# A 512-column product for both parts of the tokens, and full tiles in the retention

## Chip, core and metric

The kernel runs on one core of one Trainium2 chip. The metric is device time in microseconds: the median of 3 runs was 1045.59 us (1044.72 to 1046.28).

## The reference

Two transformer-like blocks, one after the other, on 256 tokens of width 1024, all in float32. The first puts 16 learned tokens in front (272 tokens), normalises, projects with one wide matrix, and mixes two branches: a chunkwise retention with 8 heads (rotary q and k, a decay per head, a norm and a gate) and a gated linear recurrence behind a short convolution; both are projected, gated, added and projected again (`w_out`), with a residual. A gated feed-forward of width 2816 follows. The second block projects its normalised input for a gated linear attention (4 heads), a sparse attention that keeps the 64 best keys by an indexer's scores (8 heads), and an attention on 256 memory rows; three gates merge them, and a mixture of 16 experts (two chosen per token) ends the block.

In short, of each projection:

```
proj = u @ w_in                      # u: tokens x 1024, float32
s = einsum(q, k) * intra             # retention, per head and chunk
out = einsum(s, v) + cross           # cross: through the carried state
```

## The kernel before, in words

Tokens lie transposed: features in the 128 partitions (8 tiles of 128 for the width), tokens in the columns. Float32 accuracy is had from the fast float32r products by splitting every operand in a high and a low part: weights by `_emit` (a ScalarE copy to float32r at L268, a VectorE subtraction at L269), tokens by `split_act` (L299 and L300, with a scale L302 and L303). A projection is `ws` (L325): for each output tile of 128 features and each of its 8 input tiles k it issues three products into one PSUM tile of 128x512, of which 256 or 272 columns are used: weights high by tokens high (L342), weights high by tokens low (L343), weights low by tokens high (L344). Then it lets the running side jobs take a step (`self.step()`) and hands the PSUM tile to `evac`, which is the stage's own function and works on VectorE and ScalarE. `proj` (L356) calls `ws` for 256 output features, one "chunk" of weights, at a time. With `tail=n` the two output tiles of a chunk are first computed without the last n input tiles, and those are added at the end, so that the first products of a stage don't need the last tiles of the stage before.

Weights come by DMA from SP's queue as chunks of 1 MB, in two halves of 128x1024. `get` splits up to two chunks ahead (AHEAD = 2), and there are six buffers for high and six for low halves. PSUM has two pools of four tiles: `mm` for the projections and `sp` for all else. Small working tiles of at most 272 columns come from a pool of 12 buffers (`self.t`). The order of the instructions on each engine is set at build time by the framework's scheduler, from the program's order and costs and readiness that it reckons itself; where a side job is a generator, its parts are put into the program at `self.step()`, one part per output tile.

The stages in order, with the time in the profile at which they start: li (0), v, gb and the recurrence's gates (35), k and ga (99), q and g with the retention (148), lg (213), br_ret (237), br_lru (262), out1 (285), ffi (308), ffo (434), then in block 2 iq (496), sm, dq (514), dk and dv (548), gk and gq (558), gv (585), gg (607), gt0 with o_gla and gt1 with o_dsa (640), mk (745), mv (770), mq (792), gt2 (820), o_mem (856), out2 (879), and the experts (905 on).

In the retention each head has three score products: with the first chunk of 128 keys (L626), with the 16 leading tokens (L627, 16 output partitions), and with the second chunk (L628). Their results are scaled and masked to `sm`, `s1`, `s2` (L630 to L632). Later the head's output is summed from products with `sm` (L640, 16 rows), `s1` (L641) and `s2` (L643). These are plain float32 products; the profile shows two records for each.

`sp` and `mm` in a row's names are the two PSUM pools, `tmp` the small working tiles, `big` the large ones, `raw`, `hi` and `lo` the weights before and after the split.

Of the kernel before, what the change touches and what calls it, by code (L numbers as in the profile page):

```python
# [195 lines left out]


class _Build:
    def __init__(self, nc, tc, ctx, a):
# [21 lines left out]
    def bigt(self, dt=F32, shape=(P, KT, T1)):  # L221
        return self.big.tile(list(shape), dt, name=self.name("big"), tag="big")

    def t(self, n, dt=F32, tag=None):
# [99 lines left out]

    def ws(self, keys, x, evac, nk=(KT,), cols=slice(0, SEQ), ms=(P, P), bank=None, tail=0):  # L325


        nc = self.nc
        xh, xl = x
        chunks = [self.get(*k) for k in keys]  # L330
        tiles = [(c, kc) for c, n in enumerate(nk) for kc in range(n)]
        n, nt = cols.stop - cols.start, len(tiles)
        pss = [None] * len(ms)

        def products(j, ks):
            m, ps = ms[j], pss[j]
            for k in ks:
                c, kc = tiles[k]
                hi, lo = chunks[c][j]
                wh, wl = hi[:, kc * m:kc * m + m], lo[:, kc * m:kc * m + m]  # L340
                rh, rl = xh[:, k, cols], xl[:, k, cols]
                nc.tensor.matmul(ps[:m, :n], wh, rh, start=k == 0, stop=False)  # L342
                nc.tensor.matmul(ps[:m, :n], wh, rl, start=False, stop=False)  # L343
                last = nc.tensor.matmul(ps[:m, :n], wl, rh, start=False, stop=k == nt - 1)  # L344
            return last
        for j in range(len(ms)):
            if not tail or j == 0:
                for i in range(len(ms)) if tail else (j,):
                    pss[i] = (bank or self.mm)()
                    products(i, range(nt - tail))  # L350
            if tail:
                products(j, range(nt - tail, nt))
            self.step()
            evac(j, pss[j][:ms[j], :n])

    def proj(self, key, n, x, evac, cols=slice(0, SEQ), j0=0, bank=None, tail=0):  # L356

        for j in range(j0, j0 + n // 256):
            self.ws([(key, j)], x, lambda i, ps, j=j: evac(2 * j + i, ps), cols=cols, bank=bank,
                    tail=tail if j == j0 else 0)  # L360

# [70 lines left out]
    def block1(self):  # L432
# [11 lines left out]
        x = self.bigt()  # L444
        uh, ul = self.bigt(F32R), self.bigt(F32R)
        u = (uh, ul)
        self.prm = self.keep(NPRM)
# [117 lines left out]
        def turn_v(j, vf):  # L565
            pt = self.sp()
            for t in range(2):
                te.transpose(pt[:, t * P:t * P + P], vf[:, META + t * P:META + t * P + P], self.c("ident"))
            te.transpose(pt[:META, 2 * P:3 * P], vf[:, 0:META], self.c("ident"))
            act.copy(vt[:, :, j, :], pt[:, 0:2 * P].rearrange("p (t e) -> p t e", t=2))  # L570
            act.copy(vm[:META, j, :], pt[:META, 2 * P:3 * P])
        def ev_gate(dst):
# [7 lines left out]
        for j in range(4):  # L580
            if j:
                lru(j - 1)
            convolve(j)
            self.proj("v", 256, u, ev_v, cols=ALL, j0=j)
            self.proj("gb", 256, u, ev_gate(tb), cols=X, j0=j)

# [20 lines left out]
        for j in range(4):  # L607
            self.proj("k", 256, u, rot(k, ALL), cols=ALL, j0=j)
            self.proj("ga", 256, u, ev_gate(ta), cols=X, j0=j)
# [5 lines left out]
        yh, yl = self.bigt(F32R, (P, KT, SEQ)), self.bigt(F32R, (P, KT, SEQ))  # L615
        qd = self.c("qdec").rearrange("p (t h) -> p t h", t=2)
# [4 lines left out]
        def retention(h0):  # L621
            ss = self.s(4)
            parts = []
            for h in (h0, h0 + 1):
                pm, p1, p2 = self.sp(), self.sp(), self.sp()
                te.matmul(p1[:, :SEQ], k[:, h, META:META + P], q[:, h, :SEQ], start=True, stop=True)  # L626
                te.matmul(pm[:META, :SEQ], k[:, h, 0:META], q[:, h, :SEQ], start=True, stop=True)  # L627
                te.matmul(p2[:, :P], k[:, h, META + P:T1], q[:, h, P:SEQ], start=True, stop=True)  # L628
                sm, s1, s2 = self.t(SEQ), self.t(SEQ), self.t(P)
                act.mul(sm[:META, :], pm[:META, :SEQ], kd[:META, h:h + 1])  # L630
                v.scalar_tensor_tensor(s1, p1[:, :SEQ], kd[:, 8 + h:9 + h], self.c("tri1"), op0=ALU.mult, op1=ALU.mult)
                v.scalar_tensor_tensor(s2, p2[:, :P], kd[:, 16 + h:17 + h], self.c("tri"), op0=ALU.mult, op1=ALU.mult)  # L632
                parts.append((sm, s1, s2))
                yield
            po = self.sp()
            for h, (sm, s1, s2) in zip((h0, h0 + 1), parts):
                b = (h - h0) * 2 * P
                for t in range(2):
                    o = po[:, b + t * P:b + t * P + P]
                    te.matmul(o, sm[:META, t * P:t * P + P], vm[:META, h, :], start=True, stop=False)  # L640
                    te.matmul(o, s1[:, t * P:t * P + P], vt[:, 0, h, :], start=False, stop=t == 0)  # L641
                    if t:
                        te.matmul(o, s2, vt[:, 1, h, :], start=False, stop=True)  # L643
# [40 lines left out]

        rh, rl = self.bigt(F32R, (P, KT, SEQ)), self.bigt(F32R, (P, KT, SEQ))
        def ev_gelu(j, ps):
# [17 lines left out]
        nc.sync.dma_start(x, self.a["xT"][:, :, META:])  # L704
        mh, ml = self.bigt(F32R, (P, KT, SEQ)), self.bigt(F32R, (P, KT, SEQ))

# [7 lines left out]
        h1 = self.bigt(shape=(P, KT, SEQ))  # L714
        uh, ul = self.bigt(F32R, (P, KT, SEQ)), self.bigt(F32R, (P, KT, SEQ))
        acc1 = self.t(SEQ, tag="acc")
# [21 lines left out]
        late = []  # L738
        hid = [(self.bigt(F32R, (P, KT, SEQ)), self.bigt(F32R, (P, KT, SEQ))) for _ in range(3)]

        class _Hid:
            def __init__(self, i):
                self.i = i

            def __getitem__(self, key):
                p, k, cols = key
                return hid[k // 8][self.i][p, k % 8, cols]
        for j in range(NFF):
            sgt = {}

            def ev(i, ps, j=j, sgt=sgt):
# [5 lines left out]
                else:  # L757
                    z = sgt["z"]
                    v.tensor_tensor(z, ps, z, op=ALU.mult)
                    self.split_act(hid[j // 8][0][:, j % 8, :], hid[j // 8][1][:, j % 8, :], z)  # L760
            self.ws([("ffi", j)], (uh, ul), tail=0 if j else 1, evac=ev if j else lambda i, ps: late.append((i, ps)))
# [4 lines left out]
        h2 = self.bigt(shape=(P, KT, SEQ))  # L766
        vh, vl = self.bigt(F32R, (P, KT, SEQ)), self.bigt(F32R, (P, KT, SEQ))
        fg = self.keep(8)
# [9 lines left out]
        for j in range(4):  # L778
            self.ws([("ffo", j, h) for h in range(3)], (_Hid(0), _Hid(1)), lambda i, ps, j=j: ev_ffo(2 * j + i, ps),
                    nk=(8, 7, 7))  # L780
# [23 lines left out]
    def block2(self, h2, hx, acc2, acc3):  # L804
# [194 lines left out]
        def ev_dk(j, ps):  # L999
# [3 lines left out]
            self.later(self.col_sums, pss, 2 * j, sq)  # L1003
        self.proj("dk", 256, hx, ev_dk)
        pvs = [self.mm() for _ in range(2)]
# [74 lines left out]

        oh, ol = self.bigt(F32R, KS), self.bigt(F32R, KS)
        gss = self.s(8, tag="gss", bufs=1)
# [66 lines left out]
        def ev_o(i):  # L1149
# [9 lines left out]
            return ev  # L1159
        dh, dl = self.bigt(F32R, KS), self.bigt(F32R, KS)  # L1160
        for i, (nm, o) in enumerate((("gla", (oh, ol)), ("dsa", (dh, dl)))):
# [13 lines left out]
        nc.sync.dma_start(mem, self.a["memT"])  # L1175
        n_ = nh, nl = self.bigt(F32R, KS), self.bigt(F32R, KS)
        accm = self.t(SEQ, tag="acc")
# [13 lines left out]
        def ev_heads(dst, pss, scale):  # L1191
# [12 lines left out]
            return ev  # L1204
        self.proj("mk", 1024, n_, ev_heads(mk, pss, None))
        self.finish()
# [7 lines left out]
        for j in range(2):  # L1214
            self.token_major("mv", 512, n_, ev_mv, j0=j)
            for h in (2 * j, 2 * j + 1):
                pk = self.sp()
                self.spread(pk, rk[:, 2 * h:2 * h + 2])
                for e in range(2):
# [3 lines left out]
                    self.split_act(mkh[:, 2 * h + e, :], mkl[:, 2 * h + e, :], z)  # L1223
        mqh, mql = self.bigt(F32R, KS), self.bigt(F32R, KS)
        oh, ol = mqh, mql
        pss = self.sp()
        self.proj("mq", 1024, hx, ev_heads((mqh, mql), pss, mg))
        self.finish()
# [43 lines left out]
        self.finish()  # L1272
        held["g"] = self.bigt(F32R, KS), self.bigt(F32R, KS)
        ahead = iter(range(FIRST, FIRST + sum(PRE)))
# [384 lines left out]
```

## Time and profile before

| | us |
|---|---|
| median of 3 runs | 1045.59 |
| the profiled execution | 1044.04 |
| its span, first to last instruction | 1042.3 |
| TensorE busy (share of the span) | 1027.4 (99%) |
| weight loads busy, beside products | 934.2 (90%) |
| VectorE busy | 687.5 (66%) |
| ScalarE busy | 522.6 (50%) |
| GpSimd busy | 36.9 (4%) |

Products are pipelined and their ends are modelled, so an instruction's own duration (0.28 us for 256 columns) is longer than the step from its start to the next start. TensorE's granted clock is 1.00 of full speed in all stretches but the last.

### The profile page before, as it was taken

To read this page: it belongs to the slowest core of one execution; us is meant where nothing else is said; L and a number is where in the kernel's file an instruction comes from. 1 tells how busy PE (TensorE), PEld (TensorE's weight loads), DVE (VectorE), ACT (ScalarE), POOL (GpSimd) and SP (SyncE) were. 2 spreads that over 40 slices of the span, in tenths; PEclk is the share of its full clock that TensorE was granted. 3 is DMA by queue.
4 is the path that set the end of the run, shared out by engine and by line. 5 is a ranking of instruction groups with operands and counts; after the bars stand their busy time and mean duration, and the time that the engine had idled before them with its cause. 6 is when DMAs were issued, how large, how long until landed. Compare 5 with 4: busy or idle time off the path is not lost.

```text
span 1042.3 us, 19441 instructions
## 1 busy us (share of the span) xinstructions
PE 1027.4 (99%) x7801; PEld 934.2 (90%) x7801; DVE 687.5 (66%) x1271; ACT 522.6 (50%) x928; POOL 36.9 (4%) x58
## 2 busy tenths in 40 slices
PE   8999999999999999999999999999999999999996
PEld 7999998899999999999999899999999999954342
DVE  7698986667876666666698556786647668423334
ACT  6578444464455444455566456564555554221111
POOL 3200000000000000000101000000000000000000
PEclk9999999999999999999999999999999999999998
DMA  8745563446555555566535643545555467757992
GB/s 324 241 148 179 178 204 124 124 137 195 191 185 172 191 185 178 175 189 196 168 108 164 201 162 123 184 140 182 183 173 175 159 203 270 276 207 309 410 409 81
DMA packets 57475, 203.32 MB, mean 195 GB/s; under 512 B 6416, under 2 KB 7824, under 8 KB 57248
## 3 DMA queue, kind: packets, MB, share of 16 engines
q1 hardware_dynamic: 57232, 201.91, 56.8%
q8 instruction: 63, 1.03, 0.4%
q14 instruction: 36, 0.29, 0.1%
q10 hardware_dynamic: 144, 0.09, 0.0%
HBM read 200.92 MB, written 1.05 MB: 194 GB/s over the span
## 4 chain that ended last, share of the span: by engine, by line
PE 97%; DVE 1%; ACT 0%; DMA 0%; issue 0%; POOL 0%; DVEq 0%; ACTq 0%; POOLq 0%
PE mm L342 23%; PE mm L343 23%; PE mm L344 23%; PE mm L1497 5%; PE mm L1528 3%; PE mm L381 2%; PE mm L383 2%; PE mm L382 2%; PE mm L1453 1%; PE sp L403 1%; PE sp L640 1%; PE sp L1544 1%; PE sp L641 1%; PE sp L1545 1%; PE mm L524 1%; PE sp L410 0%
## 5 line engine op out<-in xcount | busy, mean ns | idle before, releaser
L342 PE MATMUL mm<-big,hi 128*128 128x256 f32 (+1 forms) x2024 | 575.4, 284 | 0.0
L344 PE MATMUL mm<-big,lo 128*128 128x256 f32 (+1 forms) x2024 | 569.5, 281 | 0.0
L343 PE MATMUL mm<-big,hi 128*128 128x256 f32 (+1 forms) x2024 | 569.3, 281 | 0.0
L268 ACT ACTIVATE hi<-raw 128x1024 fp32r<-128x1024 f32 (+1 forms) x279 | 292.6, 1052 | 290.1 <-PE mm L343 162.8
L269 DVE TENSOR_TENSOR lo<-raw,hi 128x1024 fp32r<-128x1024 f32 (+1 forms) x279 | 338.5, 1215 | 119.1 <-ACT hi L268 115.8
L342 PEld LDWEIGHTS mm<-big,hi 128*128 128x128 f32 x2024 | 381.3, 188 | 1.7 <-issue 1.0
L343 PEld LDWEIGHTS mm<-big,hi 128*128 128x128 f32 x2024 | 381.1, 188 | 0.7 <-DVE big L303 0.2
L344 PEld LDWEIGHTS mm<-big,lo 128*128 128x128 f32 x2024 | 380.4, 188 | 0.0
L397 POOL TENSOR_TENSOR sml<-sml,keep 128x2 f32<-128x2 f32 (+4 forms) x17 | 19.4, 1142 | 672.7 <-DVE sml L842 188.8
L1506 DVE SCALAR_TENSOR_TENSOR tmp<-mm,sml,tmp 128x256 f32<-128x256 f32 x8 | 3.9, 484 | 42.6 <-ACT tmp L1505 42.6
L381 PE MATMUL mm<-hi,big 128*128 128x512 f32 (+1 forms) x80 | 29.9, 374 | 0.0
L383 PE MATMUL mm<-lo,big 128*128 128x512 f32 (+1 forms) x80 | 29.7, 372 | 0.0
L382 PE MATMUL mm<-hi,big 128*128 128x512 f32 (+1 forms) x80 | 29.6, 370 | 0.0
L299 ACT ACTIVATE tmp<-mm 128x512 fp32r<-128x512 f32 x16 | 9.5, 597 | 32.5 <-PE mm L1528 28.9
L1505 ACT ACTIVATE tmp<-mm,sml 128x256 f32<-128x256 f32 x8 | 3.8, 474 | 42.7 <-PE mm L1497 42.7
L300 DVE TENSOR_TENSOR tmp<-mm,tmp 128x512 fp32r<-128x512 f32 x16 | 10.9, 690 | 17.2 <-ACT tmp L299 16.7
L1497 PE MATMUL mm<-raw,big 128*64 128x512 f32 x96 | 21.3, 592 | 0.0
L1547 DVE TENSOR_TENSOR big<-sp,big 128x512 f32<-128x512 f32 x32 | 19.8, 679 | 2.2 <-PE sp L1545 2.2
L299 ACT ACTIVATE big<-tmp 128x256 fp32r<-128x256 f32 x46 | 18.2, 406 | 5.8 <-DVE tmp L690 3.2
L1497 PE MATMUL mm<-exp,big 128*64 128x512 f32 x96 | 21.1, 592 | 0.0
L1497 PEld LDWEIGHTS mm<-raw,big 128*64 128x64 f32 x96 | 6.9, 137 | 13.7 <-issue 13.4
L1497 PEld LDWEIGHTS mm<-exp,big 128*64 128x64 f32 x96 | 6.9, 137 | 13.7 <-issue 12.6
(389 smaller groups left out, 1138.5 us busy)
## 6 DMA issues: line engine op xcount, KB each, us to landing
raw<-w SPq DMA_DIRECT2D x289, 512.0 KB, 3.6
exp<-w SPq DMA_DIRECT2D x44, 512.0 KB, 10.1
big<-w SPq DMA_DIRECT2D x28, 512.0 KB, 7.0
raw<-w SPq DMA_DIRECT2D x16, 448.0 KB, 3.2
big<-xT SPq DMA_DIRECT2D x4, 272.0 KB, 4.4
big<-xT SPq DMA_DIRECT2D x1, 1024.0 KB, 6.2
big<-memT SPq DMA_DIRECT2D x1, 1024.0 KB, 5.7
out<-big SPq DMA_DIRECT2D x4, 256.0 KB, 4.2
```

What stands on the lines that cost most here:

```text
L268: nc.scalar.activation(hi[:, :n], raw[:, :n], AF.Copy)
L269: nc.vector.tensor_tensor(lo[:, :n], raw[:, :n], hi[:, :n].bitcast(F32), op=ALU.subtract)
L299: nc.scalar.activation(hi, src, AF.Copy)
L342: nc.tensor.matmul(ps[:m, :n], wh, rh, start=k == 0, stop=False)
L343: nc.tensor.matmul(ps[:m, :n], wh, rl, start=False, stop=False)
L344: last = nc.tensor.matmul(ps[:m, :n], wl, rh, start=False, stop=k == nt - 1)
L381: nc.tensor.matmul(ps[:, :w], xh[:, k, c], wh, start=k == 0, stop=False)
L382: nc.tensor.matmul(ps[:, :w], xl[:, k, c], wh, start=False, stop=False)
L383: nc.tensor.matmul(ps[:, :w], xh[:, k, c], wl, start=False, stop=k == last)
L1497: mm = te.matmul(ps[j * SLOTS:j * SLOTS + SLOTS, :], xg[h][k // 4][:, k % 4, o + j * SLOTS:o + j * SLOTS + SLOTS], w[:, kc * 512:kc * 512 ...
L1528: mm = te.matmul(pd[b][j * SLOTS:j * SLOTS + SLOTS, :], hf[:, k * P + j * SLOTS:k * P + j * SLOTS + SLOTS], w[:, b * 512:b * 512 + 512], s ...
L1547: v.tensor_tensor(y[:, t, c], ps, (base if p == 0 else y)[:, t, c], op=ALU.add)
```

## The change

`ws` gets `merge`. Where it is on, the output has 256 columns, no tail and two full output tiles, the high and the low part of the tokens lie side by side in one tile ([P, 4, 2, n]: 4 input tiles, 2 parts, n tokens), and one product of the weights' high part with 512 columns replaces L342 and L343; it fills the whole PSUM tile. The product of the weights' low part with the tokens' high part goes to the first 256 columns, and for all input tiles but the first it is issued ahead of the 512-column one. After the last product ScalarE copies the second half of the PSUM tile to a new working tile, VectorE adds the first half to it, and `evac` gets that working tile instead of PSUM.

`merge=False` is passed for gb, ga, dk, the last quarter of mk and mq, and the last quarter of out2. Calls with 272 columns (li, v, k), with a tail (the first chunk of out1, ffi, o_gla, o_dsa, o_mem, out2) or with one output tile (sm) stay as they were too. All token operands of these stages are allocated by `pair`, in the same number of large tiles as before.

In the retention the score product with the 16 leading tokens takes the first 128 keys instead of 16, its scaling works on 128 partitions (kdec is zero from row 16 on), and the output products with `sm` have 128 rows; the transpose of v's leading tokens and its copy are widened in the same way.

```diff
+class _Part:
+    def __init__(self, tiles, i):
+        self.tiles, self.i = tiles, i
+    def __getitem__(self, key):
+        p, k, cols = key
+        return self.tiles(k)[p, k % 4, self.i, cols]
...
+    def pair(self, n=SEQ):
+        tiles = [self.bigt(F32R, (P, 4, 2, n)) for _ in range(2)]
+        return tuple(_Part(lambda k: tiles[k // 4], i) for i in range(2))
...
+        merge = merge and n == SEQ and not tail and ms == (P, P)
         def products(j, ks):
             m, ps = ms[j], pss[j]
+            out = ps[:m, :n]
             for k in ks:
...
-                rh, rl = xh[:, k, cols], xl[:, k, cols]
-                nc.tensor.matmul(ps[:m, :n], wh, rh, start=k == 0, stop=False)
-                nc.tensor.matmul(ps[:m, :n], wh, rl, start=False, stop=False)
-                last = nc.tensor.matmul(ps[:m, :n], wl, rh, start=False, stop=k == nt - 1)
-            return last
+                first, last = k == 0, k == nt - 1
+                if not merge:
+                    nc.tensor.matmul(out, wh, xh[:, k, cols], start=first, stop=False)
+                    nc.tensor.matmul(out, wh, xl[:, k, cols], start=False, stop=False)
+                    nc.tensor.matmul(out, wl, xh[:, k, cols], start=False, stop=last)
+                else:
+                    both = ps[:m, 0:2 * n].rearrange("p (i n) -> p i n", i=2), wh, xh.tiles(k)[:, k % 4, :, cols]
+                    part = out, wl, xh[:, k, cols]
+                    for args in (both, part) if first else (part, both):
+                        nc.tensor.matmul(*args, start=first and args is both, stop=last and args is both)
...
-            evac(j, pss[j][:ms[j], :n])
+            ps = pss[j][:ms[j], :n]
+            if merge:
+                both, ps = pss[j], self.t(n)
+                nc.scalar.copy(ps, both[:, n:2 * n])
+                nc.vector.tensor_tensor(ps, both[:, 0:n], ps, op=ALU.add)
+            evac(j, ps)
...
-            te.transpose(pt[:META, 2 * P:3 * P], vf[:, 0:META], self.c("ident"))
+            te.transpose(pt[:, 2 * P:3 * P], vf[:, 0:P], self.c("ident"))
-            act.copy(vm[:META, j, :], pt[:META, 2 * P:3 * P])
+            act.copy(vm[:, j, :], pt[:, 2 * P:3 * P])
...
-                te.matmul(pm[:META, :SEQ], k[:, h, 0:META], q[:, h, :SEQ], start=True, stop=True)
+                te.matmul(pm[:, :SEQ], k[:, h, 0:P], q[:, h, :SEQ], start=True, stop=True)
-                act.mul(sm[:META, :], pm[:META, :SEQ], kd[:META, h:h + 1])
+                act.mul(sm, pm[:, :SEQ], kd[:, h:h + 1])
...
-                    te.matmul(o, sm[:META, t * P:t * P + P], vm[:META, h, :], start=True, stop=False)
+                    te.matmul(o, sm[:, t * P:t * P + P], vm[:, h, :], start=True, stop=False)
...
-        self.proj("dk", 256, hx, ev_dk)
+        self.proj("dk", 256, hx, ev_dk, merge=False)
...
-        self.proj("mk", 1024, n_, ev_heads(mk, pss, None))
+        for j in range(4):
+            self.proj("mk", 256, n_, ev_heads(mk, pss, None), j0=j, merge=j < 3)
...
-            self.proj("out2", 256, held["g"], ev_out, j0=j, tail=0 if j else 1)
+            self.proj("out2", 256, held["g"], ev_out, j0=j, tail=0 if j else 1, merge=j < 3)
```

## Rows read from the trace of the kernel before

**Rows 1.** The page's busy times: us, share of the span, instructions.

```profile
PE 1027.4 (99%) x7801; PEld 934.2 (90%) x7801; DVE 687.5 (66%) x1271; ACT 522.6 (50%) x928; POOL 36.9 (4%) x58
```

**Rows 2.** The chain that ended last, by engine.

```profile
PE 97%; DVE 1%; ACT 0%; DMA 0%; issue 0%; POOL 0%; DVEq 0%; ACTq 0%; POOLq 0%
```

**Rows 3.** Timeline of TensorE, ffi: start, duration, operation, shape (first and nineteenth).

```profile
400.22 0.28 PE L344 MATMUL mm<-big,lo 128*128 128x256 f32 x1
...
402.34 0.28 PE L344 MATMUL mm<-big,lo 128*128 128x256 f32 x1
```

**Rows 4.** The same, mv: the first of nine 512-column products, and what follows.

```profile
789.63 0.39 PE L381 MATMUL mm<-hi,big 128*128 128x512 f32 x1
...
791.71 0.27 PE L410 MATMUL sp<-keep,sml 128*128 128x128 f32 x1
```

**Rows 5.** Groups of instructions by line and shape, TensorE.

```profile
L342 PE MATMUL mm<-big,hi 128*128 128x256 f32 x1864 | 528.8, 284 | 0.0
```

**Rows 6.** Timeline of TensorE, retention: a head's score products, and what follows.

```profile
157.02 0.59 PE L626 MATMUL sp<-big,big 128*128 128x256 f32 x2
157.55 0.60 PE L627 MATMUL sp<-big,big 128*16 128x256 f32 x2
...
158.33 0.36 PE L342 MATMUL mm<-big,hi 128*128 128x256 f32 x1
```

**Rows 7.** The same: a head's output products, from the product ahead of them.

```profile
165.36 0.28 PE L344 MATMUL mm<-big,lo 128*128 128x256 f32 x1
165.57 0.48 PE L640 MATMUL sp<-big,tmp 16*128 16x128 f32 x2
165.98 0.49 PE L641 MATMUL sp<-big,tmp 128*128 128x128 f32 x2
...
167.28 0.37 PE L342 MATMUL mm<-big,hi 128*128 128x256 f32 x1
```

**Rows 8.** Timeline of TensorE, sparse attention: float32 products on full tiles.

```profile
647.75 0.38 PE L1051 MATMUL sp<-big,big 128*128 128x128 f32 x2
647.97 0.60 PE L1052 MATMUL sp<-big,big 128*128 128x256 f32 x2
...
658.34 0.60 PE L1073 MATMUL sp<-tmp,big 128*128 128x256 f32 x2
658.77 0.38 PE L1074 MATMUL sp<-tmp,big 128*128 128x128 f32 x2
658.91 0.36 PE L342 MATMUL mm<-big,hi 128*128 128x256 f32 x1
```

**Rows 9.** Busy us by stretch (k and ga; br_lru), then clock, DMA share, GB/s.

```profile
105.00:145.00 40.00, 40.00 (x332) 40.00 (x332) 37.95 (x65) 19.09 (x23) 0.00 (x0) 1.00 0.61 194
...
262.00:285.00 23.00, 23.00 (x197) 23.00 (x196) 18.78 (x31) 11.24 (x16) 0.00 (x0) 1.00 0.56 184
```

**Rows 10.** Timelines of VectorE and ScalarE, br_lru: one output tile's evacuation.

```profile
273.22 0.42 DVE L709 SCALAR_TENSOR_TENSOR tmp<-big,mm 128x256 f32<-128x256 f32 x1 [0.26 <-PE mm L344]
273.68 0.42 DVE L710 TENSOR_TENSOR tmp<-tmp,big 128x256 f32<-128x256 f32 x1
274.24 1.23 DVE L269 TENSOR_TENSOR lo<-raw,hi 128x1024 fp32r<-128x1024 f32 x1
275.38 0.42 DVE L303 SCALAR_TENSOR_TENSOR big<-tmp,big 128x256 fp32r<-128x256 f32 x1
...
273.15 1.06 ACT L268 ACTIVATE hi<-raw 128x1024 fp32r<-128x1024 f32 x1 [1.43 <-PE mm L343]
```

**Rows 11.** Timelines, ffo to iq: evacuation of the last tile, products, a ScalarE copy.

```profile
495.80 0.42 DVE L773 TENSOR_TENSOR big<-mm,keep 128x256 f32<-128x256 f32 x1 [0.28 <-PE mm L344]
...
498.07 0.39 PE L342 MATMUL mm<-big,hi 128*128 128x256 f32 x2
498.50 0.39 PE L343 MATMUL mm<-big,hi 128*128 128x256 f32 x1
...
499.94 0.35 ACT L858 COPY big<-mm 128x256 f32<-128x256 f32 x1
```

More of the change, by code (lines that the diff above doesn't have):

```diff
@@ L322, in later, with ws @@
         self.start(g())
-    def ws(self, keys, x, evac, nk=(KT,), cols=slice(0, SEQ), ms=(P, P), bank=None, tail=0):
+    def ws(self, keys, x, evac, nk=(KT,), cols=slice(0, SEQ), ms=(P, P), bank=None, tail=0, merge=True):
         nc = self.nc
@@ L353, in ws, with proj @@
             self.step()
-            evac(j, pss[j][:ms[j], :n])
-    def proj(self, key, n, x, evac, cols=slice(0, SEQ), j0=0, bank=None, tail=0):
+            ps = pss[j][:ms[j], :n]
[4 more added lines that the diff above has]
+            evac(j, ps)
+    def proj(self, key, n, x, evac, cols=slice(0, SEQ), j0=0, bank=None, tail=0, merge=True):
         for j in range(j0, j0 + n // 256):
             self.ws([(key, j)], x, lambda i, ps, j=j: evac(2 * j + i, ps), cols=cols, bank=bank,
-                    tail=tail if j == j0 else 0)
+                    tail=tail if j == j0 else 0, merge=merge)
     def exact(self, ps, terms):
@@ L444, in block1 @@
         x = self.bigt()
-        uh, ul = self.bigt(F32R), self.bigt(F32R)
-        u = (uh, ul)
+        u = uh, ul = self.pair(T1)
         self.prm = self.keep(NPRM)
@@ L584, in block1 @@
             self.proj("v", 256, u, ev_v, cols=ALL, j0=j)
-            self.proj("gb", 256, u, ev_gate(tb), cols=X, j0=j)
+            self.proj("gb", 256, u, ev_gate(tb), cols=X, j0=j, merge=False)
         RC, RS = self.c("rc"), self.c("rs")
@@ L608, in block1 @@
             self.proj("k", 256, u, rot(k, ALL), cols=ALL, j0=j)
-            self.proj("ga", 256, u, ev_gate(ta), cols=X, j0=j)
+            self.proj("ga", 256, u, ev_gate(ta), cols=X, j0=j, merge=False)
             for f in (2 * j, 2 * j + 1):
@@ L612, in block1 @@
                 v.tensor_tensor_scan(r[:, f, :], a[:, f, :], lin[:, f, 3:], 0.0, op0=ALU.mult, op1=ALU.add)
-        yh, yl = self.bigt(F32R, (P, KT, SEQ)), self.bigt(F32R, (P, KT, SEQ))
+        yh, yl = self.pair()
         qd = self.c("qdec").rearrange("p (t h) -> p t h", t=2)
@@ L682, in block1 @@
             self.proj("g", 256, u, ev_silu, cols=X, j0=j)
-        rh, rl = self.bigt(F32R, (P, KT, SEQ)), self.bigt(F32R, (P, KT, SEQ))
+        rh, rl = self.pair()
         def ev_gelu(j, ps):
@@ L704, in block1 @@
         nc.sync.dma_start(x, self.a["xT"][:, :, META:])
-        mh, ml = self.bigt(F32R, (P, KT, SEQ)), self.bigt(F32R, (P, KT, SEQ))
+        mh, ml = self.pair()
         def ev_lru(j, ps):
@@ L714, in block1 @@
         h1 = self.bigt(shape=(P, KT, SEQ))
-        uh, ul = self.bigt(F32R, (P, KT, SEQ)), self.bigt(F32R, (P, KT, SEQ))
+        uh, ul = self.pair()
         acc1 = self.t(SEQ, tag="acc")
@@ L738, in block1 @@
         late = []
[L739 to L747, printed above, removed]
+        parts = [self.bigt(F32R, (P, 4, 2, SEQ)) for _ in range(6)]
+        hid = tuple(_Part(lambda k: parts[k // 4], i) for i in range(2))
         for j in range(NFF):
@@ L759, in ev @@
                     v.tensor_tensor(z, ps, z, op=ALU.mult)
-                    self.split_act(hid[j // 8][0][:, j % 8, :], hid[j // 8][1][:, j % 8, :], z)
+                    self.split_act(hid[0][:, j, :], hid[1][:, j, :], z)
             self.ws([("ffi", j)], (uh, ul), tail=0 if j else 1, evac=ev if j else lambda i, ps: late.append((i, ps)))
@@ L766, in block1 @@
         h2 = self.bigt(shape=(P, KT, SEQ))
-        vh, vl = self.bigt(F32R, (P, KT, SEQ)), self.bigt(F32R, (P, KT, SEQ))
+        vh, vl = self.pair()
         fg = self.keep(8)
@@ L778, in block1 @@
         for j in range(4):
-            self.ws([("ffo", j, h) for h in range(3)], (_Hid(0), _Hid(1)), lambda i, ps, j=j: ev_ffo(2 * j + i, ps),
+            self.ws([("ffo", j, h) for h in range(3)], hid, lambda i, ps, j=j: ev_ffo(2 * j + i, ps),
                     nk=(8, 7, 7))
@@ L1078, in block2 @@
         self.token_major("gv", 1024, hx, lambda j, t, ps: act.mul(gv[:, t, j * 512:j * 512 + 512], ps, rb[:, t:t + 1]))
-        oh, ol = self.bigt(F32R, KS), self.bigt(F32R, KS)
+        oh, ol = self.pair()
         gss = self.s(8, tag="gss", bufs=1)
@@ L1159, in ev_o @@
             return ev
-        dh, dl = self.bigt(F32R, KS), self.bigt(F32R, KS)
+        dh, dl = self.pair()
         for i, (nm, o) in enumerate((("gla", (oh, ol)), ("dsa", (dh, dl)))):
@@ L1175, in block2 @@
         nc.sync.dma_start(mem, self.a["memT"])
-        n_ = nh, nl = self.bigt(F32R, KS), self.bigt(F32R, KS)
+        n_ = nh, nl = self.pair()
         accm = self.t(SEQ, tag="acc")
@@ L1223, in block2 @@
                     self.split_act(mkh[:, 2 * h + e, :], mkl[:, 2 * h + e, :], z)
-        mqh, mql = self.bigt(F32R, KS), self.bigt(F32R, KS)
+        mqh, mql = self.pair()
         oh, ol = mqh, mql
         pss = self.sp()
-        self.proj("mq", 1024, hx, ev_heads((mqh, mql), pss, mg))
+        for j in range(4):
+            self.proj("mq", 256, hx, ev_heads((mqh, mql), pss, mg), j0=j, merge=j < 3)
         self.finish()
@@ L1272, in block2 @@
         self.finish()
-        held["g"] = self.bigt(F32R, KS), self.bigt(F32R, KS)
+        held["g"] = self.pair()
         ahead = iter(range(FIRST, FIRST + sum(PRE)))
```

## The prediction

> **What bounds the kernel now.** I read the page's busy times first: TensorE is busy 1027.4 us, 99% of the span [rows 1], and the chain that ended last is TensorE for 97% [rows 2]. So a nanosecond taken from TensorE's stream counts, and an added VectorE or ScalarE instruction costs only where TensorE comes to wait for it. A busy TensorE need not be a fast one, so next I read its timeline for the step from one start to the next. In a long run of 256-column products 18 steps take 402.34 - 400.22 = 2.12 us, 0.1178 us each; in the products with 512 moving columns nine steps take 791.71 - 789.63 = 2.08 us, 0.2311 us each [rows 3, 4]. Twice 0.1178 less 0.2311 is 0.0045 us: what an instruction costs beyond its columns. There are 1864 triples of 256 columns [rows 5].
>
> In the retention the steps are longer than the columns ask for. The three score products of a head hold TensorE from 157.02 to 158.33, 1.31 us [rows 6]; the five output products, two of them with 16 rows, from 165.57 to 167.28, 1.71 us, and the step into them is 0.21 instead of 0.118 [rows 7]. Elsewhere the same float32 products on all 128 rows and columns take 0.43 for 256 columns, 0.22 for 128, and 0.14 for 128 when a fast product follows [rows 8]. Lastly the table of busy times by stretch: VectorE is busy 37.95 of 40 us in the k stage while TensorE is busy all 40, and 18.78 of 23 in br_lru [rows 9]. A VectorE that is 95% full does not hold TensorE up.
>
> **The change, part by part.**
>
> *Full tiles in the retention.* At the full tiles' durations a head's scores take 0.43 + 0.43 + 0.14 = 1.00 us, 0.31 less; its outputs 4 x 0.22 + 0.14 = 1.02, 0.69 less; the step into them 0.09 less. That is 1.09 us a head and 8.7 us for eight, all on TensorE [rows 6 to 8]. The ends: 0, if the long steps came from something other than the 16-row and 16-column shapes, and 9.3, if some entries lose more; I take 8.7, since the lengthening stands only beside those shapes. The wider kdec product, v transpose and copy keep their length in the free dimension and add work only on lanes that idled: nothing is taken, and ScalarE's slack hides it.
>
> *Side by side.* Of the 1864 triples those of gb, ga, dk, the last quarter of mk and mq, two quarters of out2, the four other calls that keep a tail (out1, ffi, both o of gla and dsa, o_mem: five in all) and sm stay: 18 calls of 16 triples and 8, 296 in all. 1568 triples, in 182 output tiles, become a 512- and a 256-column product: 0.0045 us x 1568 = 7.0 us less [rows 3 to 5]. The moving operand is now two stretches of 256 columns, which no row shows. The ends are no gain (the two stretches cost as two instructions, 0.236) and 0.0055, by the rounding of the two steps, 8.6 us; I take the 512-column row.
>
> The Trainium skill, page TensorE: Matmul & The Clock Gate, section Back-to-back issue gap, gives columns over 2.4 GHz plus a fixed 2.5 ns for each matmul. By that the merge is worth 2.5 ns x 1568 = 3.9 us instead of 7.0 (an estimate from that page); the rows here show 4.5 ns, and I keep them.
>
> *What it adds.* Each of 182 tiles gets a ScalarE copy out of PSUM, 0.35 [rows 11], and a VectorE add, 0.42 as L709 [rows 10]: 64 and 76 us of work. Over the span VectorE goes from 687.5 to 764 of some 1030, ScalarE from 522.6 to 586 [rows 1]. Hardest pressed is br_lru: 18.78 + 8 x 0.42 = 22.1 us in 22.7, 97%, close to the k stage's 95%. The weight splits run two chunks of 5.6 us ahead, so a backlog of a few us there reaches no product, and PSUM holds four output tiles. So no throughput loss is taken.
>
> The latency of a tile grows more. ScalarE starts a 1.06 us weight split just as a tile ends (it waits for that tile's products to free the buffer) [rows 10], and the copy can stand behind it: 0.35 + 0.42 = 0.8 us at best, 1.06 + 0.35 + 0.42 = 1.8 at worst. Queued behind the waiting add on VectorE are the low split of the weights and the tile's own operations; who waits for those is TensorE where the next projection reads the tile at once:
> - ffo to iq. The last tile is read out at 495.80 and iq's product for it starts at 498.50, after others at 498.07 and (in step) 498.19, some 0.2 late already [rows 11]. So it has no slack. The low part is now asked for one product (0.12) later. Loss 0.7 to 1.7, I take 1.2.
> - br_lru to out1, out1 to ffi, o_mem to out2. The reader does 14 triples first, 14 x 0.353 = 4.9 us, and the tile's evacuation takes 2.6 now, 273.22 to 275.80 [rows 10], and up to 4.4 then. Loss 0 to 1 each; I take 0.4 each, 1.2.
> - dq's squares, summed on TensorE one tile (2.8 us) later, after split, copy, add, low split, multiply and square, at worst 1.06 + 0.35 + 0.42 + 1.23 + 2 x 0.42 = 3.9 less what overlaps, 3.6. Loss 0 to 0.8 in each of 8 tiles; I take 0.1 each, 0.8, since the build's order can place the sums among products.
>
> Sum on the span: -8.7 - 7.0 + 1.2 + 1.2 + 0.8 = -12.5. The profiled execution took 1044.04 (its span 1042.3 and 1.7 around it), so 1031.5; the median of the runs lies 1.55 above the profiled one: 1033.1, rounded to 1033. With all losses at their upper ends, 1.7 + 3 + 6.4 = 11.1, it is 1041; with none and the gains at their upper ends, 17.9, it is 1028.
>
> **Rivals.**
> 1. *Two stretches cost as two.* Only the retention pays: 1045.6 - 8.7 + 3.2 = 1040. For it: no row has a moving operand in two pieces. Against: the step is linear in columns, with only 4.5 ns a piece to lose, and the lengths lie row by row in memory.
> 2. *A smaller fixed cost.* If only about half of the 4.5 ns is the instruction's own, the merge gives 2.25 ns x 1568 = 3.5 and the time is 1045.6 - 8.7 - 3.5 + 3.2 = 1036.6. For it: the 4.5 is a small difference of two steps read to 0.01 us over 9 and 18. Against: those roundings allow only about 1 ns either way. The Trainium skill's rule above (TensorE: Matmul & The Clock Gate, Back-to-back issue gap) would make it 1036.2.
> 3. *The evacuation's order makes VectorE the bound: slower.* In each tile VectorE would wait for split and copy, 1.06 + 0.35, before the add, with its own low split behind it. The place is ffi, 42 merged tiles in a row. Its work a tile there is 1.23 for the low split, 0.63 for evacuation (three 0.42 operations for two tiles) and 0.42 for the add, 2.28; with 1.41 idle 3.69 against TensorE's 2.8, 0.9 more a tile, 38 us, less the 11 us by which splits run ahead: 27. Then 1045.6 - 15.7 + 27 + 3.2 = 1060. It loses to before from 0.57 us a tile, an idle wait of 1.1 of the 1.41. For it: the split sits ahead on ScalarE [rows 10]. Against: the low split needs only the split, so VectorE can do it while the copy runs, and 95% in the k stage cost nothing [rows 9].
>
> **How the numbers follow.** What a measurement of this kernel can tell from no change is about 0.2%, 2 us. Forecast 1033, its own range 1029 to 1039: 0.74. Rival 2, 1037: 0.07. Rival 1, 1040: 0.06. Rival 3 in all degrees: 0.13, of which 0.04 ends within 2 us of before and 0.09 above. So faster 0.87, same 0.04, slower 0.09; the range 1028 to 1041 leaves out rival 3 and little else.
>
> **What would show it.** Right: the first product of a merged triple followed by the next start 0.231 later and the second by 0.118; scores and outputs of a head at about 1.0 us each; the new copy and add 182 times, with VectorE near 760 us and TensorE still 98% or more of the span; a wait of about 1 us at iq. Wrong: a step near 0.236 or above for the 512-column product; a full-tile head that keeps 1.3 and 1.7; several us in the list of waits from TensorE on VectorE or ScalarE in ffi, br_lru or dq.

## The result, and the profile after

The changed kernel takes 1031.37 us, the median of four runs (1030.72 to 1031.62), against 1045.93 for the kernel before (1044.72 to 1046.76): a ratio of 0.9856, 95% interval 0.9845 to 0.9868, or 14.6 us less. The forecast was 1033, between 1028 and 1041. The profiled execution took 1031.62, its span 1029.4.

The busy times and the chain by engine, answering to [rows 1, 2], and the groups that answer to [rows 5] with the two that are new (columns: busy us, mean ns of one, idle time before):

```profile
PE 1014.9 (99%) x6233; PEld 858.9 (83%) x6233; DVE 754.7 (73%) x1453; ACT 577.7 (56%) x1110; POOL 37.9 (4%) x58
...
PE 95%; DVE 2%; ACT 1%; DMA 1%; issue 1%; POOL 0%; SPq 0%; DVEq 0%; ACTq 0%; POOLq 0%
...
L368 PE MATMUL mm<-big,hi 128*128 128x512 f32 x1568 | 552.4, 398 | 0.0
L368 PE MATMUL mm<-big,lo 128*128 128x256 f32 x1568 | 409.6, 280 | 0.0
...
L380 ACT COPY tmp<-mm 128x256 f32<-128x256 f32 x182 | 67.2, 369 | 126.3 <-PE mm L368 126.0
...
L381 DVE TENSOR_TENSOR tmp<-mm,tmp 128x256 f32<-128x256 f32 x182 | 76.6, 421 | 51.5 <-ACT tmp L380 51.2
```

1568 products of 512 columns stand in the place of 3136 of 256. The copy and the add came 182 times each, 67.2 and 76.6 us where 64 and 76 were forecast, and VectorE is at 754.7 us. TensorE is still busy 99% of the span: what was added lies beside it, but for the losses counted below. A new cost would show in the list of waits. Here is its head for TensorE (who waited, for whom: us, times, longest):

```profile
PE mm L551 <- DVE big L488: 1.7, 2, 1.1
PE mm L544 <- DVE sml L470: 1.0, 1, 1.0
PE sp L570 <- POOL sml L425: 0.7, 1, 0.7
```

All three stand in the first stages. Of the rest, 0.6 us or less each, one is in dq and one in ffi (0.3 each; 0.3 and 0.4 before the change), and none in br_lru. The weight loads that go ahead of the products have a list of their own, and these three waits there, among the longest, the kernel before doesn't have:

```profile
PEld sp L1277 <- DVE tmp L1271: 0.4, 1, 0.4
PEld sp L431 <- DVE tmp L458: 0.4, 1, 0.4
PEld sp L431 <- DVE tmp L1223: 0.3, 1, 0.3
```

L431 sums the squares of the memory rows, at 737 us, and of mk, at 744, and L1277 is a transpose in the memory's attention, at 815. Next, TensorE's timeline in ffi, answering to [rows 3, 4] (start, duration, operation, shape):

```profile
399.88 0.40 PE L368 MATMUL mm<-big,hi 128*128 128x512 f32 x1
400.11 0.28 PE L368 MATMUL mm<-big,lo 128*128 128x256 f32 x1
400.23 0.39 PE L368 MATMUL mm<-big,hi 128*128 128x512 f32 x1
...
403.36 0.40 PE L368 MATMUL mm<-big,hi 128*128 128x512 f32 x1
```

From 399.88 to 403.36 ten pairs pass, 0.348 us each, against 3 x 0.1178 = 0.353 before. The 512-column product, with its operand in two stretches, is followed 0.23 later, the 256-column one 0.12 later. The retention, answering to [rows 6, 7]: a head's scores, the outputs of the first head of a pair, and those of the second:

```profile
158.41 0.59 PE L653 MATMUL sp<-big,big 128*128 128x256 f32 x2
...
159.41 0.48 PE L368 MATMUL mm<-big,hi 128*128 128x512 f32 x1
...
166.19 0.38 PE L668 MATMUL sp<-big,tmp 128*128 128x128 f32 x2
166.41 0.39 PE L669 MATMUL sp<-big,tmp 128*128 128x128 f32 x2
...
167.22 0.48 PE L368 MATMUL mm<-big,hi 128*128 128x512 f32 x1
...
168.18 0.49 PE L668 MATMUL sp<-big,tmp 128*128 128x128 f32 x2
168.50 0.39 PE L669 MATMUL sp<-big,tmp 128*128 128x128 f32 x2
...
169.32 0.48 PE L368 MATMUL mm<-big,hi 128*128 128x512 f32 x1
```

Scores hold TensorE 1.00 us (1.31 before), outputs 1.03 (1.71), and in the second head 1.14: its first product takes 0.32 where 0.22 was reckoned. Last, busy time by stretch, answering to [rows 9]; the columns are those there:

```profile
104.00:144.00 40.00, 40.00 (x332) 40.00 (x331) 39.18 (x67) 19.73 (x24) 0.00 (x0) 1.00 0.56 182
254.00:277.00 23.00, 23.00 (x135) 20.20 (x134) 21.22 (x39) 14.03 (x25) 0.00 (x0) 1.00 0.55 184
```

VectorE went from 18.78 to 21.22 of 23 us in br_lru, and TensorE lost nothing there. In the k stage, where nothing is merged, the row isn't the same stretch as in [rows 9]: the stage stands 1.6 us later in this trace, and over 106.6 to 146.6 VectorE is busy 38.03, as before.

**Where the time went.** I compared the starts of the same products in both traces, after less before. The changed kernel is late by 1.39 us at the first score product of the retention, since this execution's start lost 1.74: the first four loads of x landed a median 6.2 us after their issue, 4.4 before. (The other traces with the merge began 0.5 to 1.4 earlier than this one, but for the run with the ends apart, in which the clock fell at the start.) Over the retention the shift falls by 8.85 us, 0.55 of which is merging in the projections there. From there to the start of ffi it falls by 0.54, over ffi, ffo and iq by 2.8; over dq it rises by 0.17, and from dq to the last stage it falls by 1.4. At the last product it is -11.9; the span fell by 12.9, since what follows that product's start took 9.2 us instead of 10.2.

### The profile page after: what moved, and what is told of

Its sections match the earlier page's. It is cut to its first block, busy times and chain, and to the rows that moved or that the text cites. A ratio compares the mean times of both kernels' runs of the same rounds, so it can differ in the third digit from the quotient of the medians.

```text
span 1029.4 us, 16602 instructions
## 1 busy us (share of the span) xinstructions
PE 1014.9 (99%) x6233; PEld 858.9 (83%) x6233; DVE 754.7 (73%) x1453; ACT 577.7 (56%) x1110; POOL 37.9 (4%) x58
## 4 chain that ended last, share of the span: by engine, by line
PE 95%; DVE 2%; ACT 1%; DMA 1%; issue 1%; POOL 0%; SPq 0%; DVEq 0%; ACTq 0%; POOLq 0%
PE mm L368 52%; PE mm L360 5%; PE mm L1520 5%; PE mm L361 5%; PE mm L362 5%; PE mm L1551 3%; PE mm L409 2%; PE mm L411 2%; PE mm L410 2%; PE mm L1476 1%; PE sp L431 1%; PE sp L1567 1%; PE sp L1568 1%; DMA big<-xT 1%; PE mm L551 1%
## 5 line engine op out<-in xcount | busy, mean ns | idle before, releaser
L368 PE MATMUL mm<-big,hi 128*128 128x512 f32 x1568 | 552.4, 398 | 0.0
L368 PE MATMUL mm<-big,lo 128*128 128x256 f32 x1568 | 409.6, 280 | 0.0
L368 PEld LDWEIGHTS mm<-big,hi 128*128 128x128 f32 x1568 | 286.5, 188 | 54.5 <-issue 0.7
L380 ACT COPY tmp<-mm 128x256 f32<-128x256 f32 x182 | 67.2, 369 | 126.3 <-PE mm L368 126.0
L360 PE MATMUL mm<-big,hi 128*128 128x256 f32 (+1 forms) x456 | 130.5, 287 | 0.0
L361 PE MATMUL mm<-big,hi 128*128 128x256 f32 (+1 forms) x456 | 129.5, 284 | 0.0
L362 PE MATMUL mm<-big,lo 128*128 128x256 f32 (+1 forms) x456 | 128.9, 283 | 0.0
L381 DVE TENSOR_TENSOR tmp<-mm,tmp 128x256 f32<-128x256 f32 x182 | 76.6, 421 | 51.5 <-ACT tmp L380 51.2
L361 PEld LDWEIGHTS mm<-big,hi 128*128 128x128 f32 x456 | 85.9, 188 | 0.5 <-DVE big L318 0.2
L360 PEld LDWEIGHTS mm<-big,hi 128*128 128x128 f32 x456 | 85.8, 188 | 0.1
L410 PE MATMUL mm<-hi,big 128*128 128x512 f32 (+1 forms) x80 | 29.7, 371 | 0.0
```

What stands on the lines that cost most here:

```text
L360: nc.tensor.matmul(out, wh, xh[:, k, cols], start=first, stop=False)
L361: nc.tensor.matmul(out, wh, xl[:, k, cols], start=False, stop=False)
L362: nc.tensor.matmul(out, wl, xh[:, k, cols], start=False, stop=last)
L368: nc.tensor.matmul(*args, start=first and args is both, stop=last and args is both)
L380: nc.scalar.copy(ps, both[:, n:2 * n])
L381: nc.vector.tensor_tensor(ps, both[:, 0:n], ps, op=ALU.add)
```

## The experiments

Each ratio is to the kernel before, timed on the same chip; the changed kernel had its own repeat in the first set. What a run lies above or below the changed kernel is the difference of the medians, to 1031.97 in the first set and to 1031.37 in the later ones. Each median is known to about 1.4 us, so differences under 2 us are read from the traces, by the starts of the same products.

**The changed kernel again.** No edit.

> The changed kernel again, beside the others on one chip. Expected 1031 us, 14 to 15 less than before. Its profiled run showed the first projection starting 1.7 us later than before, behind the load of x; if that is chance, it is gone or different here.

Measured: 1031.97 us (1030.54 to 1032.57), ratio 0.9861 (0.9847 to 0.9875). It is the yardstick for the next three. Its start was 0.6 us late instead of 1.74.

**Full tiles alone.** The kernel before, with only the retention's part of the change:

```
-te.matmul(pm[:META, :SEQ], k[:, h, 0:META], q[:, h, :SEQ], ...)
+te.matmul(pm[:, :SEQ], k[:, h, 0:P], q[:, h, :SEQ], ...)
...
-te.matmul(o, sm[:META, t * P:t * P + P], vm[:META, h, :], ...)
+te.matmul(o, sm[:, t * P:t * P + P], vm[:, h, :], ...)
```

> The kernel before with the full tiles in the retention alone. My theory (the two parts add up, each on TensorE): 8.3 us less than before, about 1037.5, with 1.04 us less a head in the trace. Rival (part of the retention's gain only shows because the merged stages leave room): less than 6.

Measured: 1037.34 us, ratio 0.9920 (0.9908 to 0.9932): 8.7 less. In the trace the retention falls by 7.96, 1.0 a head.

**Side by side alone.** The changed kernel with those lines as they were.

> The changed kernel with the retention's 16-row and 16-column products as before. My theory: the merge's 7 us less some 1.5 to 2 us of waits, so 5 to 6 less than before, about 1040. Rival (the waits eat it): within 2 us of before.

Measured: 1039.19 us, ratio 0.9937 (0.9924 to 0.9950): 6.85 less. The two parts alone give 15.5, together 14.1 in the same set, each known to about 1.4: within that they add up.

**The tiles side by side, but two instructions.** The pair is kept in the same layout, with copy and add; only the product is issued in two halves, except for the first and the last of a tile (1204 more instructions):

```
-for args in (both, part) if first else (part, both):
+one = out, wh, xh[:, k, cols]
+two = ps[:m, n:2 * n], wh, xl[:, k, cols]
+for args in (both, part) if first else (part, both) if last else (part, one, two):
```

> The changed kernel, same layout, same copy and add after each tile, but for all input tiles except the first and the last of an output tile the 512-column product is issued as two of 256 columns: 1204 instructions more. My theory (what is saved is a fixed 4.5 ns an instruction): 1204 x 0.0045 = 5.4 us more than the changed kernel, about 1036.8. Rival (the gain comes from elsewhere, the layout or the order low part first): within 1 us of the changed kernel. By the skill's 2.5 ns (TensorE: Matmul & The Clock Gate, Back-to-back issue gap) it would be 3.0 us more.

Measured: 1038.02 us, ratio 0.9925 (0.9913 to 0.9938), 6.05 above the changed kernel: 5.0 ns for each instruction, with the weight load that goes with it. So the number of instructions carries the gain, not the layout or the order, and rival 2 (2.25 ns, 2.7 us here) falls. The trace has 5.3 ns on the whole, but unevenly: 10 in ffi, where all products of that execution stand further apart (last section), and 2.5 in ffo. So 5.0 is a mean; that it is one fixed cost everywhere isn't shown.

The Trainium skill, page TensorE: Matmul & The Clock Gate, section Back-to-back issue gap, has 2.5 ns as that cost, for a product by itself with no weight load counted; this run measures twice as much as the mean in a stream of both, and the measurement decides.

**Only the 16-row output products back.** The scores stay full.

```
-te.matmul(o, sm[:, t * P:t * P + P], vm[:, h, :], ...)
+te.matmul(o, sm[:META, t * P:t * P + P], vm[:META, h, :], ...)
```

> The changed kernel with only the retention's output products by 16 rows again; the scores keep full tiles. My theory: each head's outputs go back from 1.03 to 1.71 us and the step into them from 0.118 or 0.231 to 0.1 more, 0.7 to 0.8 a head, 5.5 to 6.2 us more than the changed kernel. Rival (it is the switch of 16 output columns in the scores that costs): no more than 2.5.

Measured: 1036.26 us, ratio 0.9916 (0.9902 to 0.9930), 4.9 above the changed kernel. The trace loses 0.69 us a head. TensorE's timeline there, a head's outputs:

```profile
164.62 0.40 PE L368 MATMUL mm<-big,hi 128*128 128x512 f32 x1
164.94 0.48 PE L668 MATMUL sp<-big,tmp 16*128 16x128 f32 x2
165.36 0.49 PE L669 MATMUL sp<-big,tmp 128*128 128x128 f32 x2
165.78 0.48 PE L668 MATMUL sp<-big,tmp 16*128 16x128 f32 x2
...
166.66 0.48 PE L368 MATMUL mm<-big,hi 128*128 128x512 f32 x1
```

The step into the first 16-row product is 0.32 instead of 0.23, and the next three products take 0.42 each instead of 0.22, the full one among them as long as its 16-row neighbours: 1.72 a head again. Rows change four times in this head (into 16, out, in, out), and 0.09 + 0.69 = 0.78 us over four changes is 0.2 each. The Trainium skill, page TensorEngine Tiling (Array Packing), section Key Properties, says that changing the tiling mode drains the engine. The trace fits that and has a price, which the page doesn't give; which mode a 16-row product runs in, and whether the engine is drained, it doesn't show.

**The same edit at another place.** The gated linear attention's decay products have 16 rows in both kernels; here their operands are filled with zeros and they run on 128 rows:

```
+nc.gpsimd.memset(ix[:, 6:8, :], 0.0)
+nc.gpsimd.memset(sm[64:P, :], 0.0)
...
-te.matmul(pz[:, :SEQ], a2[32:48, h * P:h * P + P], sm[32:48, :], ...)
+te.matmul(pz[:, :SEQ], a2[:, h * P:h * P + P], sm, ...)
```

> The changed kernel with the four 16-row products of the decay rates in the gated attention on all 128 rows, the added rows zero (two more memsets on GpSimd, hidden). My theory (a change of the rows in use costs about 0.1 us each time it happens, wherever it is): 0.5 to 0.6 us less in the trace at these products, too little for the times; no drop of the clock in the dq stage as the second look at the changed kernel had. Rival: no step changes.

Measured: 1030.94 us, ratio 0.9863 (0.9849 to 0.9878), not to be told from the changed kernel by time. TensorE's timelines tell it: the last decay product and what follows, first in the changed kernel, then here:

```profile
529.87 0.69 PE L967 MATMUL sp<-big 16*128 16x256 f32 x2
530.49 0.50 PE L368 MATMUL mm<-big,hi 128*128 128x512 f32 x1
```

```profile
528.41 0.59 PE L969 MATMUL sp<-big 128*128 128x256 f32 x2
528.66 0.58 PE L368 MATMUL mm<-big,hi 128*128 128x512 f32 x1
```

From start to next start 0.62 us against 0.25, of which the next product gives 0.1 back. Over all four of these products, three of them in a row, the shift falls by 0.62 us, some 0.16 for each of the four changes of rows. One widened shape gave nothing: the transpose of v's leading tokens, on 16 columns before, is followed 0.03 us later in both kernels, and over the whole v stage the shift stays within 0.05.

**Merge everywhere.** All that the change leaves apart by `merge=False` or `merge=j < 3` (gb, ga, dk, the last quarters of mk, mq and out2) is merged:

```
-self.proj("dk", 256, hx, ev_dk, merge=False)
+self.proj("dk", 256, hx, ev_dk)
...
-            self.proj("out2", 256, held["g"], ev_out, j0=j, tail=0 if j else 1, merge=j < 3)
+            self.proj("out2", 256, held["g"], ev_out, j0=j, tail=0 if j else 1)
```

> The changed kernel with the merge also in gb, ga, dk and the last quarters of mk, mq and out2: 192 triples more in 12 calls, 24 tiles. By the count alone 192 x 0.005 = 1.0 us less than the changed kernel. My theory: gb and ga give their 0.6; in the other four the squares stand 0.8 to 1.8 us later in front of the sums that TensorE waits for, some 1 us lost at each of mk, mq and out2; together 1 to 3 us more than the changed kernel. Rival (latency is hidden there as in iq): 1 us less.

Measured: 1033.89 us, ratio 0.9895 (0.9880 to 0.9909), 2.5 above the changed kernel. Two waits of TensorE are new in the list:

```profile
PE sp L431 <- ACT tmp L1023: 1.5, 2, 1.1
PE sp L1325 <- DVE big L1314: 1.3, 1, 1.3
```

L431 sums the squares of dk's last tile, which ScalarE (L1023) makes after copy and add; L1325 is the router's product for out2's last tile. The starts of products show 1.9 us lost at the end of dk and 1.1 at the end of out2, nothing at mk and mq, and 0.5 gained by gb and ga: 2.5 together, as by time. So the exceptions pay for dk and out2 and cost a little for gb and ga.

**A second VectorE operation.** Each added add is followed by one more operation of its size that changes nothing, 182 in all:

```
 nc.vector.tensor_tensor(ps, both[:, 0:n], ps, op=ALU.add)
+nc.vector.tensor_tensor(ps, ps, ps, op=ALU.max)
```

> The changed kernel with one more VectorE operation of 256 columns after each of the 182 adds (the maximum of the tile with itself), 76 us more work on VectorE, some 830 us of 1030, and 0.42 us more latency a tile. My theory (TensorE is the bound, splits run two chunks ahead): at most 3 us more than the changed kernel. Rival (VectorE is at the edge of being the bound): 10 us or more.

Measured: 1042.0 us, ratio 0.9968 (0.9957 to 0.9980), 10.6 above the changed kernel. My bound of 3 fell; the price is the rival's. But it isn't paid in the long run of tiles in ffi. VectorE's share in ffi, changed kernel first, then this one (columns as in [rows 9]):

```profile
310.00:420.00 110.00, 110.00 (x634) 95.91 (x633) 88.58 (x141) 70.34 (x122) 0.00 (x0) 1.00 0.57 187
```

```profile
310.00:420.00 110.00, 109.18 (x630) 94.78 (x629) 96.67 (x175) 66.93 (x121) 0.70 (x1) 1.00 0.56 181
```

VectorE does 8 us more in these 110. The shift against the changed kernel is 5.38 us at 317 and 5.36 at 504: all of ffi and ffo lose nothing. It grows by 1.7 in the retention, by 4.7 from out1 to the start of ffi, by 2.1 at the start of gv, and by 2.8 from mk into the memory's attention; in dq it falls by 0.5. The waits there:

```profile
PE mm L410 <- DVE tmp L381: 1.8, 1, 1.8
PE sp L1278 <- DVE tmp L1272: 1.3, 1, 1.3
...
PE mm L361 <- DVE big L318: 0.9, 1, 0.9
```

L361 is ffi's product for the tile that out1 has just finished, and L1278 transposes attention weights that VectorE has just scaled: a tile is read at once. Some 1.7 of the 4.7 is the clock (last section). The longest wait is another kind: L410 is gv's product, which writes a PSUM tile, and L381 is the add that still has to read that tile for gq. VectorE is busy without a break from 573 to 583 there. In the retention too a score product waits for a PSUM tile that VectorE (L660) has still to read, its weight load for 0.6 and 0.8 us. So VectorE had room over the long run of tiles in ffi; it had none where a tile is read at once, nor where it fell so far behind that PSUM tiles came free late (some 3.8 us, in the retention and at gv), and there the rival was right.

**The ends apart.** The tiles that the next projection reads first are three products again (92 triples), so they have no copy and add:

```
-self.proj("br_lru", 1024, (rh, rl), ev_lru)
+self.proj("br_lru", 768, (rh, rl), ev_lru)
+self.proj("br_lru", 256, (rh, rl), ev_lru, j0=3, merge=False)
...
-                    nk=(8, 7, 7))
+                    nk=(8, 7, 7), merge=j < 3)
```

and so with out1 and o_mem.

> The changed kernel with the last quarters of br_lru, out1, ffo and o_mem as three products again, 92 triples (44 in ffo, 16 in each other); so the tiles that the next projection reads at once have no copy and add. Prediction's losses (iq 1.2, three transitions 1.2 together): it gains 2.4 and pays 92 x 0.005 = 0.5, so 1.9 us below the changed kernel, 1029.5. Rival (the ledger of the two traces shows no loss at these places, since other products are ready there): only the 0.5 us are paid, 1031.9; in the trace the shift against the changed kernel is +0.1 over br_lru, +0.1 over out1, +0.2 over ffo, +0.1 over o_mem and no step back at iq.

Measured: 1030.67 us (1029.34 to 1033.76), ratio 0.9859 (0.9840 to 0.9878): by time no difference, and too wide to part 1029.5 from 1031.9. By the starts of the same instructions, the shift against the changed kernel goes from +0.13 to +0.12 over br_lru, to -0.15 by the first tiles of ffi, from there to -0.07 by iq, and by +0.04 over o_mem. The added instructions should cost 0.08, 0.08, 0.22 and 0.08 there. So the ends gave back 0.1, 0.4, 0.1 and less than 0.1, 0.6 together. The prediction had 2.4, the rival none: the rival is nearer, but for out1.

**The parts that paid, together.** gb and ga merged as well, and the decay products on full tiles.

> The changed kernel with gb and ga side by side too (32 tiles... 16 for the two projections, 8 triples each less) and the decay products of the indexer on full tiles. From the traces of the two parts run apart: gb and ga gave 0.5 us of the span between the start and the first retention score, the decay products 0.7, with no loss behind either. Theory (gains of parts that meet on no common engine wait add up): 1.2 us below the changed kernel, 1030.2, ratio to before 0.985. Rival 1 (the k stage, where VectorE was busy 37.95 of 40 us, is at its edge once four more copies and adds a quarter stand there and only looked free): 1 to 3 us above the changed kernel. Rival 2 (the decay products' gain is spread between executions and not a gain): equal to the changed kernel, within 0.5 us.

Measured: 1029.25 us (1028.77 to 1029.73), ratio 0.9841 (0.9827 to 0.9855), 16.4 us under before, and some 2 under the changed kernel, the lowest of all runs (by time the step from the changed kernel isn't shown: the intervals of the two ratios overlap). In the trace gb and ga give 0.5 and the decay products 0.7, as apart. VectorE is the fullest here of all:

```profile
104.00:144.00 40.00, 40.00 (x271) 37.21 (x270) 39.66 (x72) 20.56 (x29) 0.00 (x0) 1.00 0.54 171
```

39.66 of 40 us, and TensorE still busy all 40.

## Why the prediction was right, term by term

**Retention, 8.7 forecast.** 8.7 measured by time and 8.0 in the trace of the part alone. Scores and entry were sized right. The output term was 0.1 too large in the second head of each pair, whose first product keeps a step of 0.32 (its weight load waits 0.2 for ScalarE): [rows 7] are those of a first head, and I took all eight from it.

**Merge, 7.0 forecast.** 6.85 measured by time for this part alone, its losses included, and 5.5 in its trace; with the losses the forecast was 7.0 - 3.2 = 3.8. An instruction costs 5.0 ns beyond its columns by the added instructions, 5.0 by the shift in ffi (1.6 us over 323 triples), 4.5 by [rows 3, 4]. Over two stretches the operand costs as much as over one, so rival 1 falls.

**VectorE's throughput, no loss forecast.** Right for the change in the places named: no new wait in br_lru, and 0.2 in ffi. It was nearer the edge than "two chunks ahead" made it sound: a second operation of 0.42 a tile costs 10 us, where a tile is read at once and, for some 3.8, where VectorE frees PSUM tiles too late. Rival 3 had the place wrong too; ffi is where nothing is lost.

**Latency at the ends, 2.4 forecast (iq 1.2, three transitions 1.2).** This is the step that failed: 0.6 were there, 0.1 of it at iq. I feared that the copy would queue behind a weight split. Timelines of ScalarE, VectorE and TensorE from ffo to iq, answering to [rows 11]:

```profile
485.10 0.37 ACT L380 COPY tmp<-mm 128x256 f32<-128x256 f32 x1 [1.37 <-PE mm L368]
485.36 1.07 ACT L283 ACTIVATE hi<-raw 128x1024 fp32r<-128x1024 f32 x1
...
485.50 0.42 DVE L381 TENSOR_TENSOR tmp<-mm,tmp 128x256 f32<-128x256 f32 x1 [0.52 <-ACT tmp L380]
...
487.89 0.48 DVE L318 SCALAR_TENSOR_TENSOR big<-big,keep,big 128x256 fp32r<-128x256 f32 x1
...
487.12 0.39 PE L368 MATMUL mm<-big,hi 128*128 128x512 f32 x1
487.44 0.38 PE L368 MATMUL mm<-big,lo 128*128 128x256 f32 x1
...
488.36 0.27 PE L368 MATMUL mm<-big,lo 128*128 128x256 f32 x1
488.47 0.68 PE L368 MATMUL mm<-big,hi 128*128 128x512 f32 x2
```

The copy goes ahead of the split: both wait for the tile's last product and the copy stands first in ScalarE's order. The split is then what is late, and it has chunks in hand. TensorE loses 0.24 us here, the step of 0.32 from 487.12 among it, where 0.23 is due; at the same place before the change it lost 0.30 already, so nothing near 1.2 was added. In br_lru the copy stands first as well, answering to [rows 10]:

```profile
262.57 0.37 ACT L380 COPY tmp<-mm 128x256 f32<-128x256 f32 x1 [0.60 <-PE mm L368]
262.84 1.06 ACT L283 ACTIVATE hi<-raw 128x1024 fp32r<-128x1024 f32 x1
```

One of the transitions does lose, out1 to ffi. TensorE, then VectorE:

```profile
301.64 0.66 PE L361 MATMUL mm<-big,hi 128*128 128x256 f32 x2
302.13 0.40 PE L362 MATMUL mm<-big,lo 128*128 128x256 f32 x2
...
300.24 1.23 DVE L284 TENSOR_TENSOR lo<-raw,hi 128x1024 fp32r<-128x1024 f32 x1
301.38 0.48 DVE L318 SCALAR_TENSOR_TENSOR big<-big,keep,big 128x256 fp32r<-128x256 f32 x1
```

Two L361 take 0.49 us, where two steps are 0.24: the second multiplies the low part of a tile whose split (L318) ends at 301.86, having stood behind the low split of the weights. These 0.25 are most of the 0.4 that came back when out1's end was left apart.

**dq's squares, 0.8 forecast.** About 0.5: the shift rises by 0.17 over dq where 64 merged triples give 0.3.

**The sum.** The profiled execution was forecast at 1031.5 and took 1031.62; that it came so close is luck. Against the forecast, the retention gave 0.4 less in this trace (8.3), the start came 1.74 late, and 0.5 more lay outside the span (2.2 for 1.7); on the other side the losses were 0.7 to 1.5 smaller, and what follows the last product's start was 0.9 shorter (other traces have 9.1 to 10.4 there, with no order by kernel). The offset of 1.55 between profile and median, which I carried over from before, does not belong to the kernel: after, the profiled execution was 0.25 above the median.

The losses: -8.3 for the retention, -7.1 to -7.8 for the merge (1568 x 4.5 to 5.0 ns) and +1.74 for the start leave 1.7 to 2.5 of loss in a shift of -11.9, where 3.2 was forecast. Of this 0.6 is at the ends and 0.5 in dq, where the prediction looked. The other 0.6 to 1.4 is in stages where it took nothing. The shift rises by 0.4 at the start of mk (742 to 758 in the trace before) and by 0.4 in the memory's attention (814 to 830), though triples are merged there too, and the new waits of the weight loads stand just there. That the added copies and adds make VectorE late for them is the likely cause; no run tests it.

What the runs support is 8.0 to 8.7 less for the retention and 7.1 to 7.8 for the merge, with 1.7 to 2.5 lost: -13.4 to -14.0, against -14.6 measured, which is known to about 1.2.

## What to carry to other kernels

Where TensorE is busy 99%, look for what its stream spends besides columns: joining two moving operands under one weight pays the fixed cost of an instruction once, and a float32 product with fewer rows or columns than its neighbours can lengthen them (a 16-column transpose here did not), so filling it up with zeros can be cheaper than it looks. An operation added to an engine with slack costs nothing in a long run of tiles, even at 95 to 99% of a stretch, but up to its whole latency where the next product reads the tile at once, and more where the engine falls behind far enough to hold PSUM tiles: look at who reads a tile first, and leave those apart. Before charging a queueing delay, see which of the two waiting instructions stands first.

## What the runs showed that I had not expected

TensorE's granted clock fell to half, 1.2 GHz, for 3.4 us in three of the profiled executions, each time elsewhere: in dq (the changed kernel's repeat), at the start of ffi (the second VectorE operation), and in the first stage (the ends apart). Busy time and granted clock by 2 us of the last of these (columns as in [rows 9]):

```profile
16.00:18.00 2.00, 1.30 (x10) 0.91 (x10) 0.32 (x3) 0.00 (x0) 1.15 (x3) 1.00 1.04 416
18.00:20.00 2.00, 2.00 (x13) 1.85 (x12) 2.00 (x5) 1.51 (x4) 0.92 (x1) 0.70 1.01 404
20.00:22.00 2.00, 2.00 (x11) 2.00 (x11) 1.98 (x6) 2.00 (x5) 1.75 (x3) 0.50 0.93 317
```

In the next 2 us the clock is 0.95. TensorE was idle for 0.7 of 2 us just ahead. It cost 1.55 us by the starts of products. The changed kernel's first profile has the same idle stretch (busy 1.30 of 18 to 20) and no fall, and in dq the engine counted as busy throughout the 4 us ahead, with small products: what decides isn't settled.

With only the retention changed, the products of ffi, the same in both kernels, stood 1.1 ns further apart each, 1.2 us in all, and in the run with two instructions some 1.2 ns. Why is open. An unexplained ns a product is a quarter of the cost that the merge saves, so the 4.5 to 5.0 ns are means over stages and not a constant.
